# Hymba layer, both feed-forward products: seven block products in both halves, the second one product by product over all channels, weight sums stored

## The chip, the cores and the metric

One core of a Trainium2 chip. The metric is device time in microseconds for one execution of the whole program; lower is better. Before the change three runs gave a median of 2140.09 us.

## What is computed (the reference, cut)

One decoder layer over 2048 tokens (16 meta tokens are put ahead and removed again), model width 1024, all in float32:

```python
s = layer_norm(concat(meta, x), ln_in_g, ln_in_b)
u = s @ w_in                       # columns: conv value, conv gate, q, k, v, output gate, forget gate
conv_out = silu(layer_norm(depthwise_conv31(val * sigmoid(gate)) + conv_b))   # 512 channels
gla_out  = rms_norm(gated_linear_attention(q, k, v, log_g)) * silu(r)         # 4 heads, chunks of 64
s = layer_norm(ALPHA * s + concat(conv_out, gla_out) @ w_out, ln1_g, ln1_b)
f = square(relu(s @ w_ff1)) @ w_ff2          # 1024 -> 4096 -> 1024
out = layer_norm(ALPHA * s + f, ln2_g, ln2_b)
```

## The kernel before, in words

**Precision.** TensorE multiplies in a reduced float32 form. Each operand is therefore split into a high part (a cast on ACT, L189) and the rest (a subtraction on DVE, L190), and each product is three matmuls, high by high, high by low, low by high, that add up in one PSUM bank.

**Tiling.** The tokens are four sub-blocks s = 0..3 of 512; two of them are a *half* (half 0 is s = 0, 1; half 1 is s = 2, 3). The order on the chip is: input projection, attention and convolution of all four; then for each half the output projection (`wout_units`), the first feed-forward product (FF1 below) and the second (FF2). `stats`/`late` are the sums of a layer norm whose application is put off into FF1.

**FF1.** An ordinary product of one half is 2 x 2 blocks by 2 x 2 blocks, eight block products. Half 0 does these (`ff1_units`, `ff1_unit`): 16 groups of 256 channels, 4 units each of 24 matmuls of 128x512, 1536 in all. `put_left` then forms the seven left operands that FF2 wants, already split, and stores them (`hod`). Half 1 uses the scheme with seven block products and more additions (`ff1s_units`): 16 groups x 7 products x 12 matmuls, 1344. There products 1 and 2 of the first ten groups (NFR = 10, "the front") run ahead while a side generator (`back_units`) makes the operands X3 to X7 of the others; product 1 of each front group is kept in SBUF (`a1`, 10 buffers), and the seven left operands of FF2 are stored unsplit (`hor`).

**FF2.** In both halves seven block products (`ff2_units`). The 4096 inner channels are four groups q; a *block* is one product i of one group, with i in the order 1, 7, 5, 6, 2, 3, 4, so that there are 28 blocks, and in each 4 units (tt, 128 tokens each) of 12 matmuls: 48 per block, 1344 per half. Before, the blocks run group by group: each unit starts a new bank, and every bank is at once added into accumulators in SBUF (112 evacuations a half, L1251, L1253, L1256). The residual ALPHA*s is added in at the first group. The right operands are the quadrants of w_ff2 (11, 12, 21, 22), loaded once per group (`raw_load`, L1185) and combined in place by 32 DVE subtractions a half (`sub`, L1202). Left operands come from `hod` (half 0) or are loaded from `hor` (`raw_left`, L1159 for blocks 0 and 1, L1163 for later ones) and split (`load_left`, half 1).

**What sets the order.** `prog.add` makes units with a cost; `prog.load` hands weight tiles out of a ring of 10 slots of 512 KB (pool `wp`, tiles `wr`, `w1r`, `wop`); `prog.side` spreads the steps of a generator between two marks, by cost; `prog.defer` puts a step off. A scheduler then fixes each engine's order when the program is built, and the engines run that order: an instruction that waits holds all behind it on its engine. Loads are issued by SP; some stores by ACT. The convolution of sub-block s, `conv(s)`, is such a side generator: 120 `scalar_tensor_tensor` on DVE (L729) with a layer norm over channels, which needs 32 transposes on TensorE (L736, L750).

Of the kernel before, what the change touches and what calls it, by code (L numbers as in the profile page):

```python
# [10 lines left out]
F32 = mybir.dt.float32  # L11
# [134 lines left out]
def hymba_kernel(ctx: ExitStack, tc: tile.TileContext, x, meta, ln_in_g, ln_in_b, w_in, small, gate_up,  # L146
# [639 lines left out]
    def load_ln2():  # L786
        for nm_, src in (("g2", ln2_g), ("b2", ln2_b)):
# [95 lines left out]

    def put_left(half, g, i, t):
        o = B.f1.tile([P, 2, SUB], F32R, tag="ho", name="ho", bufs=6)
        split(o[:, 0, :], o[:, 1, :], t)
        nc.sync.dma_start(out=hod[half][g // GP][i - 1][:, g % GP, :, :].bitcast(F32), in_=o.bitcast(F32))

    hr = {}

    def ff1_unit(s, g, m, ls):
        half, i = divmod(s, 2)
        ps = mm_tile()
        ch_matmul(ps, ls, m, lambda k, hl: xs(st1[s], k, hl))
        t = hr[i, m] = B.f1.tile([P, SUB], F32, tag="hr", name="hr", bufs=8)
        nc.scalar.activation(t, ps, AF.Relu)  # L898
        nc.scalar.activation(t, t, AF.Square)
        if i == 0:  # L900
            put_left(half, g, 1 + m, t)
        if (i, m) == (1, 1):
            a11, a12, a21, a22 = hr[0, 0], hr[0, 1], hr[1, 0], hr[1, 1]
            put_left(half, g, 4, a22)
            s3 = B.f1.tile([P, SUB], F32, tag="s3", name="s3", bufs=2)
            sub = lambda o, x, y: nc.vector.tensor_tensor(out=o, in0=x, in1=y, op=ALU.subtract)
            sub(s3, a11, a21)
            put_left(half, g, 7, s3)
            nc.vector.tensor_tensor(out=a21, in0=a21, in1=a22, op=ALU.add)
            put_left(half, g, 5, a21)  # L910
            sub(a21, a21, a11)
            put_left(half, g, 6, a21)
            sub(a21, a12, a21)
            put_left(half, g, 3, a21)

    def ff1_units(half, tail):
        for g in range(NG):
            l1 = loads_ch(w1, g * G * P)
            for i in range(2):
                for m in range(G):  # L920
                    prog.add(lambda s=2 * half + i, g=g, m=m, l1=l1: ff1_unit(s, g, m, l1), l1, 5.2)
                if i == 0 and g == NG - 1:
                    tail()

# [64 lines left out]
    def ff1s_units(half, stats, f2):  # L989
# [61 lines left out]
        def put(g, i, t, late=False):  # L1051
            o = hor[g // GP][i - 1][:, g % GP, :]
# [9 lines left out]
        bank = {}  # L1062

        def unit(g, i, l):
# [5 lines left out]
            st = bank  # L1070
            if i == 1:
                a1[g] = B.f1.tile([P, SUB], F32, tag="a1", name="a1", bufs=10)
                nc.scalar.copy(a1[g], ps)
            elif i == 2:
# [43 lines left out]
        prog.add(open_h, cost=0.01)  # L1118
# [13 lines left out]
        prog.add(lambda: open_x(True), cost=0.01)  # L1132
        f2.head2()
# [3 lines left out]
    def op_tile(n, r):  # L1137
        if n % 5 == r:
            return B.x.tile([P, GP, 2, SUB], F32R, tag="ox", name="ox")
        return xtp.tile([P, GP, 2, SUB], F32R, tag="xt", name="op")  # L1140

    def ff2_units(half, f2):
        seq = [(q, i) for q in range(NGR) for i in ORDER]
        lt, rt, accs, sums, raws = {}, {}, {}, {}, {}
        count = [0]

        def nxt():
            count[0] += 1
            return op_tile(count[0] - 1, 4 if half else 2)

        stage = {}

        def raw_left(n):
            if half and n < len(seq):
                q, i = seq[n]
                if n < 2:
                    stage[n] = [B.f1.tile([P, SUB], F32, tag="a1", name="lr", bufs=10) for _ in range(GP)]
                    for p in range(GP):
                        nc.sync.dma_start(out=stage[n][p], in_=hor[q][i - 1][:, p])  # L1159
                else:  # L1160
                    stage[n] = [B.acc.tile([P, 2, SUB], F32, tag="lr", name="lr", bufs=4) for _ in range(GP // 2)]
                    for u in range(GP // 2):
                        nc.sync.dma_start(out=stage[n][u], in_=hor[q][i - 1][:, 2 * u:2 * u + 2])  # L1163

        def load_left(n):
            if half:
                if n < len(seq):
                    lt[n] = nxt()
                    for u, r in enumerate(stage[n]):
                        w = GP // len(stage[n])  # L1170
                        o = lt[n][:, u * w:(u + 1) * w]
                        split(o[:, :, 0, :], o[:, :, 1, :], r.rearrange("p (k t) -> p k t", k=1) if w == 1 else r)
            elif n < len(seq):
                q, i = seq[n]
                lt[n] = nxt()
                for p in range(GP):
                    nc.sync.dma_start(out=lt[n][:, p].bitcast(F32), in_=hod[half][q][i - 1][:, p].bitcast(F32))

        def raw_load(q, j, k, u):
            def fn():  # L1180
                t = wp.tile([P, 2, 512], F32, tag="w", name="wr")
                if j is not None:
                    r0 = (q * GP + 2 * u) * G * P
                    src = w2[r0:r0 + 2 * G * P, k * 512:(k + 1) * 512]
                    nc.sync.dma_start(out=t, in_=src.rearrange("(a j p) c -> j p a c", a=2, j=2)[j])  # L1185
# [3 lines left out]
        def group_loads(q):  # L1189
            r = raws[q] = {}  # L1190
            for nm_, j, k in (("11", 0, 0), ("22", 1, 1), ("12", 0, 1), ("t3", None, None), ("21", 1, 0)):
                r[nm_] = [raw_load(q, j, k, u) for u in range(2)]

        needs = {1: ("11",), 7: ("22", "12", "t3"), 5: ("12", "11"), 6: ("22", "12"), 2: ("21",), 3: ("22",),
                 4: ("21", "12")}

        def right(n):
            q, i = seq[n]
            rt[n] = nxt()
            for u in range(2):  # L1200
                b11, b22, b12, t3, b21 = [prog.slot.get(raws[q][x][u]) for x in ("11", "22", "12", "t3", "21")]
                sub = lambda o, x, y: nc.vector.tensor_tensor(out=o, in0=x, in1=y, op=ALU.subtract)  # L1202
                if i == 7:
                    sub(t3, b22, b12)
                elif i == 5:
                    sub(b12, b12, b11)
                elif i == 6:
                    sub(b12, b22, b12)
                elif i == 4:
                    sub(b12, b21, b12)  # L1210
# [216 lines left out]
```

## Time and profile before

| | |
|---|---|
| three runs | 2137.29, 2140.09, 2142.95 us |
| the profiled execution | 2142.86 us, of which the trace's span is 2140.9 us (1.96 us lie around it) |
| TensorE busy | 2061.7 us, 96% of the span |
| DVE, ACT busy | 1639.6 us (77%), 970.4 us (45%) |
| DMA | 391.05 MB, mean 183 GB/s |

The profile names, for each engine, the share of time in which it had an instruction in flight. Matmuls overlap each other, so that the pace of TensorE is read from the distance of their starts, not from their durations. The first matmuls of the stages lie at: FF1 of half 0 713 us, its FF2 1073 us, output projection 2 and 3 1394 us, FF1 of half 1 1487 us, its FF2 1809 us; the last matmul starts at 2123.9 us.

### The profile page before, as it was taken

How to read it: one execution, taken by the hardware profiler on the slowest of the kernel's cores; microseconds unless marked ns; L12 is line 12 of the kernel's file. 1: busy time of each engine (PE TensorE's matmuls, PEld its weight loads, DVE VectorE, ACT ScalarE, POOL GpSimd, SP SyncE). 2: the span in 40 equal slices, each digit the busy share in tenths (PEclk: the TensorE clock that was granted, in tenths of full speed). 3: DMA queues.
4: the chain of work that ended last, by engine and by line, in shares of the span. 5: the costliest groups of instructions: out<-in, count | busy, mean ns of one | idle time of the engine just before them, and what ended most of it. 6: DMA issues, size and time to landing. Idle time of an engine off the chain costs nothing. (4 is left out here: it accounts for less than half of the span.)

```text
span 2140.9 us, 26599 instructions
## 1 busy us (share of the span) xinstructions
PE 2061.7 (96%) x9336; PEld 1687.1 (79%) x9336; DVE 1639.6 (77%) x2670; ACT 970.4 (45%) x1688; POOL 92.0 (4%) x104
## 2 busy tenths in 40 slices
PE   6999999999899999999999999899999999999995
PEld 5878878878777788888878788788777788888884
DVE  6699989989988644599645656868878776787888
ACT  3554474653543445655441312244635555533332
POOL 3000100000000000000000000011000000000002
PEclk9999999999999999999999999999999999999998
DMA  5533534434346476656796876547455547744422
GB/s 187 170 106 103 151 112 126 146 98 129 119 152 211 153 256 219 221 215 229 272 366 251 276 263 229 182 144 222 156 181 190 187 141 259 284 151 155 135 79 79
DMA packets 211654, 391.05 MB, mean 183 GB/s; under 512 B 19792, under 2 KB 103984, under 8 KB 211520
## 3 DMA queue, kind: packets, MB, share of 16 engines
q1 hardware_dynamic: 204608, 376.77, 52.4%
q10 hardware_dynamic: 6912, 12.59, 1.6%
q8 instruction: 73, 1.20, 0.2%
q14 instruction: 61, 0.50, 0.1%
HBM read 263.21 MB, written 126.07 MB: 182 GB/s over the span
## 5 line engine op out<-in xcount | busy, mean ns | idle before, releaser
L393 PE MATMUL mm<-xt,wsl 128*128 128x512 f32 x896 | 353.0, 394 | 0.7 <-ACT xt L189 0.7
L395 PE MATMUL mm<-xt,wsl 128*128 128x512 f32 x896 | 352.0, 393 | 0.0
L394 PE MATMUL mm<-xt,wsl 128*128 128x512 f32 x896 | 351.9, 393 | 0.0
L729 DVE SCALAR_TENSOR_TENSOR cacc<-hin,sm,cacc 128x512 f32<-128x512 f32 x480 | 343.6, 743 | 1.6
L189 ACT CAST wsl<-raw 128x512 fp32r<-128x512 f32 x288 | 176.9, 621 | 207.6 <-PE mm L395 57.9
L190 DVE TENSOR_TENSOR wsl<-raw,wsl 128x512 fp32r<-128x512 f32 x284 | 193.4, 689 | 62.1 <-ACT wsl L189 61.4
L1246 PE MATMUL mm<-op 128*128 128x512 f32 x544 | 213.1, 392 | 6.3 <-DVE aa L1253 6.3
L1247 PE MATMUL mm<-op 128*128 128x512 f32 x544 | 213.2, 392 | 0.9 <-DVE op L190 0.9
L1248 PE MATMUL mm<-op 128*128 128x512 f32 x544 | 212.9, 391 | 0.0
L189 ACT CAST op<-wr 128x1024 fp32r<-128x1024 f32 x92 | 92.5, 1050 | 263.7 <-PE mm L1248 151.7
L393 PEld LDWEIGHTS mm<-xt,wsl 128*128 128x128 f32 x896 | 169.2, 189 | 35.0 <-ACT xt L189 0.9
L394 PEld LDWEIGHTS mm<-xt,wsl 128*128 128x128 f32 x896 | 169.2, 189 | 34.8 <-issue 0.8
L395 PEld LDWEIGHTS mm<-xt,wsl 128*128 128x128 f32 x896 | 169.0, 189 | 34.9
L190 DVE TENSOR_TENSOR op<-wr,op 128x1024 fp32r<-128x1024 f32 x92 | 109.0, 1220 | 39.3 <-ACT op L189 39.3
L1246 PEld LDWEIGHTS mm<-op 128*128 128x128 f32 x544 | 102.8, 189 | 28.3 <-issue 6.7
L1247 PEld LDWEIGHTS mm<-op 128*128 128x128 f32 x544 | 102.7, 189 | 22.8 <-DVE op L190 1.3
L1248 PEld LDWEIGHTS mm<-op 128*128 128x128 f32 x544 | 102.7, 189 | 21.4
L190 DVE TENSOR_TENSOR ho<-hr,ho 128x512 fp32r<-128x512 f32 x96 | 64.5, 684 | 34.9 <-ACT ho L189 32.1
L242 POOL TENSOR_TENSOR rs<-rs,nhalf 128x1 f32<-128x1 f32 x46 | 41.7, 908 | 1120.3 <-DVE rs L241 1117.1
L1251 DVE TENSOR_TENSOR ac<-ac,mm 128x512 f32<-128x512 f32 x72 | 49.1, 683 | 49.3 <-PE mm L1248 49.3
L898 ACT ACTIVATE hr<-mm 128x512 f32<-128x512 f32 x64 | 38.3, 598 | 103.3 <-PE mm L395 103.3
L1246 PE MATMUL mm<-op,ox 128*128 128x512 f32 x192 | 76.3, 397 | 7.6 <-issue 5.4
(304 smaller groups left out, 4362.6 us busy)
## 6 DMA issues: line engine op xcount, KB each, us to landing
hod<-ho SPq DMA_DIRECT2D x112, 512.0 KB, 3.6
op<-hod SPq DMA_DIRECT2D x88, 512.0 KB, 5.9
raw<-in_w_in_dram SPq DMA_DIRECT2D x160, 256.0 KB, 2.9
wr<-in_w_dram SPq DMA_DIRECT2D x64, 512.0 KB, 5.8
lr<-hor SPq DMA_DIRECT2D x52, 512.0 KB, 4.8
raw<-in_w_dram SPq DMA_DIRECT2D x84, 256.0 KB, 2.9
raw<-in_w_out_dram SPq DMA_DIRECT2D x64, 256.0 KB, 3.6
w1r<-in_w_dram SPq DMA_DIRECT2D x32, 512.0 KB, 5.1
```

Source lines behind the costliest of these rows:

```text
L189: nc.scalar.copy(hi, src)
L190: (eng or nc.vector).tensor_tensor(out=lo, in0=src, in1=hi.bitcast(F32), op=ALU.subtract)
L242: nc.gpsimd.tensor_tensor(out=rs, in0=rs, in1=nhalf[:, :1], op=ALU.pow)
L393: nc.tensor.matmul(ps, wh, mov(k, 0), start=(k == 0), stop=False)
L394: nc.tensor.matmul(ps, wh, mov(k, 1), start=False, stop=False)
L395: nc.tensor.matmul(ps, wl, mov(k, 0), start=False, stop=(k == KD - 1))
L729: nc.vector.scalar_tensor_tensor(out=acc, in0=h[:, j:j + SUB], scalar=wc(j), in1=acc, op0=ALU.mult, op1=ALU.add)
L898: nc.scalar.activation(t, ps, AF.Relu)
L1246: nc.tensor.matmul(ps, lh, rt[n][:, p, 0, :], start=(p == 0), stop=False)
L1247: nc.tensor.matmul(ps, lh, rt[n][:, p, 1, :], start=False, stop=False)
L1248: nc.tensor.matmul(ps, ll, rt[n][:, p, 0, :], start=False, stop=(p == GP - 1))
L1251: add = lambda o, a, b: nc.vector.tensor_tensor(out=o, in0=a, in1=b, op=ALU.add)
```

## The change

- FF1 runs with seven block products in half 0 as well (`ff1s_units` for both halves; `ff1_units`, `put_left` and `hod` go; `hor` exists for both). `wout_units(1)` therefore leaves its layer norm to FF1 (`late[0]`).
- The front's product 1 no longer stays in SBUF: ACT stores it (`a1d`), `a1` has 5 buffers, and `reload(g)` brings it back one group ahead.
- FF2 goes through all four groups of one product before the next product. A bank per tt then collects 4 x 12 matmuls, and is emptied only at the last group: a copy on ACT for products 1, 7, 5; four DVE adds for 6; one DVE add for 2, 3, 4. The residual comes in apart from this (`res_load`, `res_add`).
- The quadrants of w_ff2 no longer stay between products. In half 0 each block loads what it needs (`parts`), one or two pieces, and where there are two, the difference is formed (32 of 128x1024), used, and stored by ACT in DRAM (`td`). Half 1 loads the stored differences.
- Only block 0's left operand is fetched ahead of FF2 (`head`); blocks 1 and 2 follow behind `open_f2`.
- `conv(2)` is spread up to the end of FF1 of half 0, `conv(3)` over FF2 of half 0; before, `conv(2)` ended a little into FF1, and `conv(3)` ran mainly in FF1.
- The gains of the last layer norm are loaded after FF2 of half 0, and the layer norm of sub-block 2 runs between the blocks of the last product.

```diff
-        seq = [(q, i) for q in range(NGR) for i in ORDER]
+        seq = [(i, q) for i in ORDER for q in range(NGR)]
...
+        if half == 0:
+            parts = {1: ("11",), 7: ("22", "12"), 5: ("12", "11"), 6: ("22", "t5"), 2: ("21",), 3: ("22",), 4: ("21", "t6")}
+        else:
+            parts = {1: ("11",), 7: ("t7",), 5: ("t5",), 6: ("t6",), 2: ("21",), 3: ("22",), 4: ("t4",)}
...
+                ops = [prog.slot[l] for l in slots[n][u]]
+                x = ops[0]
+                if len(ops) == 2:
+                    nc.vector.tensor_tensor(out=x, in0=x, in1=ops[1], op=ALU.subtract)
+                split(rt[n][:, 2 * u:2 * u + 2, 0, :], rt[n][:, 2 * u:2 * u + 2, 1, :], x)
+                if len(ops) == 2:
+                    nc.scalar.dma_start(out=td[i][q][u], in_=x)
...
-            ps = mm_tile()
+            if q == 0:
+                bank[tt] = mm_tile()
+            ps = bank[tt]
...
+            if q < NGR - 1:
+                return
             x = accs[tt]
...
+            if i in (1, 7, 5):
+                nc.scalar.copy(x.slot[i], ps)
             elif i == 6:
-                add(o, o, ps)
-                add(o, o, x.slot[1])
...
+                add(x.slot[6], x.slot[1], ps)
+                add(x.slot[7], x.slot[7], x.slot[6])
+                add(x.slot[6], x.slot[6], x.slot[5])
+                add(x.slot[5], x.slot[5], x.slot[7])
...
         def head():
             prog.add(lambda: raw_left(0), cost=0.01)
-            prog.add(lambda: raw_left(1), cost=0.01)
             prog.add(lambda: load_left(0), cost=0.01)
             add_right(0)
...
+                if n == 0:
+                    z(raw_left, 1)
+                    z(raw_left, 2)
...
-        if half:
-            ff1s_units(half, stats, f2)
-        else:
-            ff1_units(half, tail)
+        ff1s_units(half, stats, f2)
...
-    mid = m_ff0 + 30
-    prog.side(later(conv(2), 100), CONV_N, W[3].gv_end, mid)
-    prog.side(later(conv(3), 100), CONV_N, mid, m_f20 + 60)
+    prog.side(later(conv(2), 100), CONV_N, W[3].gv_end, m_f20)
+    prog.side(later(conv(3), 100), CONV_N, m_f20, m_w2 - 4)
```

The order on DVE in the middle of FF2 of half 0. Before (`aa`, `ab`, `ac` are the accumulators, `mm` a bank, `wr` weights as loaded, `op`/`ox` split operands):

```order
L1251 TENSOR_TENSOR aa<-aa,mm 128x512
L1202 TENSOR_TENSOR wr<-wr 128x1024 x2
L1251 TENSOR_TENSOR aa<-aa,mm 128x512
L1202 TENSOR_TENSOR wr<-wr 128x1024 x2
L1251 TENSOR_TENSOR aa<-aa,mm 128x512 x2
L190 TENSOR_TENSOR op<-wr,op 128x2x512 x2
L1251 TENSOR_TENSOR ab<-ab,mm 128x512 x4
```

Now, for one block of product 7 (`lr` is a left operand as loaded, `cacc` the convolution's sum):

```order
L730 SCALAR_TENSOR_TENSOR cacc<-hin,sm,cacc 128x512
L1168 TENSOR_TENSOR wr<-wr 128x1024
L730 SCALAR_TENSOR_TENSOR cacc<-hin,sm,cacc 128x512
L1168 TENSOR_TENSOR wr<-wr 128x1024
L730 SCALAR_TENSOR_TENSOR cacc<-hin,sm,cacc 128x512 x5
L191 TENSOR_TENSOR op<-wr,op 128x2x512 x2
L191 TENSOR_TENSOR op<-lr,op 128x2x512 x2
```

The additions into accumulators are gone from the block; seven convolution steps and two splits of the left operand have come in.

On SP at the passage from FF1 to FF2 in half 1. Before, block 1's left operand (`hor0_6`) follows at once on block 0's (`hor0_0`), far ahead of the stores of FF1's last results:

```order
L1159 DMA lr_15136<-hor0_0_168 128x512
L1159 DMA lr_15137<-hor0_0_168 128x512
L1159 DMA lr_15145<-hor0_6_174 128x512
L1159 DMA lr_15146<-hor0_6_174 128x512
L1159 DMA lr_15147<-hor0_6_174 128x512
L1159 DMA lr_15148<-hor0_6_174 128x512
```

Now block 1's (`hor1_1_0`) stands behind the last of these stores:

```order
L1014 DMA hor1_3_5_194<-h11_15151 128x512
L1014 DMA hor1_3_2_191<-s4_15259 128x512
L1147 DMA wr_15285<-td7_2_0_224 128x1024
L1132 DMA lr_15272<-hor1_1_0_175 128x1024
L1132 DMA lr_15273<-hor1_1_0_175 128x1024
L1132 DMA lr_15276<-hor1_2_0_182 128x1024
L1132 DMA lr_15277<-hor1_2_0_182 128x1024
```

The same stands in half 0 (`hor0_1_0` behind the stores to `hor0_3_...`). The place of block 2's load before is the place of block 1's load now.

On ACT in FF2 of half 0, where the stores to `td` are issued; casts of blocks 5 and 6 (counted from 0), now:

```order
L190 CAST op_9670<-wr_9360 128x2x512
L190 CAST op_9670<-wr_9451 128x2x512
L190 CAST op_9716<-lr_9583 128x2x512
L190 CAST op_9716<-lr_9584 128x2x512
L1171 DMA td7_3_0_226<-wr_9600 128x1024
L1171 DMA td7_3_1_227<-wr_9679 128x1024
L190 CAST op_9753<-wr_9522 128x2x512
L190 CAST op_9753<-wr_9596 128x2x512
L190 CAST ox_9797<-lr_9666 128x2x512
L190 CAST ox_9797<-lr_9667 128x2x512
L1171 DMA td5_0_0_204<-wr_9683 128x1024
L1171 DMA td5_0_1_205<-wr_9762 128x1024
```

Each store stands ahead of the casts of the block before it: `td7_3` (group 3 of product 7) is ahead of the casts from `wr_9522`, which is group 2. Before, ACT issued no stores in FF2, only casts and copies of banks.

## Rows read from the trace of the kernel before

**Rows 1.** The page: TensorE's busy time, and the clock granted in 40 slices.

```profile
PE 2061.7 (96%) x9336; PEld 1687.1 (79%) x9336; DVE 1639.6 (77%) x2670; ACT 970.4 (45%) x1688; POOL 92.0 (4%) x104
PEclk9999999999999999999999999999999999999998
```

**Rows 2.** Busy time by stage: length, PE, PEld, DVE, ACT, POOL, clock, DMA share, GB/s.

```profile
601.00:713.00 112.00, 107.49 (x520) 87.45 (x519) 84.94 (x171) 40.81 (x93) 8.59 (x8) 1.00 0.54 178
713.00:1073.00 360.00, 357.25 (x1604) 294.59 (x1603) 250.80 (x405) 193.32 (x335) 6.37 (x8) 1.00 0.64 231
1073.00:1394.00 321.00, 312.09 (x1375) 256.57 (x1374) 202.76 (x277) 89.23 (x119) 2.20 (x4) 0.99 0.73 258
1487.00:1809.00 322.00, 317.16 (x1376) 253.96 (x1376) 237.35 (x383) 169.62 (x298) 3.49 (x4) 1.00 0.55 185
1809.00:2124.00 315.00, 307.72 (x1344) 253.43 (x1342) 256.31 (x318) 122.33 (x141) 4.62 (x5) 0.99 0.43 149
2124.00:2141.00 17.00, 0.00 (x0) 0.00 (x0) 11.64 (x26) 5.52 (x9) 6.63 (x6) 0.63 0.34 130
```

**Rows 3.** Timeline of TensorE late in FF2 of half 0: start, duration, instruction.

```profile
1361.64 0.39 PE L1247 MATMUL mm<-op 128*128 128x512 f32 x1
...
1365.27 0.39 PE L1248 MATMUL mm<-op 128*128 128x512 f32 x1
1371.11 0.77 PE L1246 MATMUL mm<-op,ox 128*128 128x512 f32 x1 [5.45 <-issue]
1371.67 0.63 PE L1247 MATMUL mm<-op,ox 128*128 128x512 f32 x1
1372.10 0.63 PE L1248 MATMUL mm<-op,ox 128*128 128x512 f32 x1
```

**Rows 4.** TensorE's transposes of a convolution's layer norm, 713 to 1073 us, by line.

```profile
L750 PE MATMUL tp<-ident,cn 128*128 128x128 f32 x16 | 3.4, 280 | 0.5 <-ACT cn L747 0.5
L736 PE MATMUL tp<-ident,cacc 128*128 128x128 f32 x16 | 2.6, 272 | 0.0
```

**Rows 5.** DVE's convolution steps (L729 alone) in FF1 and FF2 of half 0.

```profile
713.00:1073.00 360.00, 84.79 (x120) 1.00 0.64 231
1073.00:1394.00 321.00, 0.00 (x0) 0.99 0.73 258
```

**Rows 6.** Timeline of DVE: two instructions back to back, of 1024 and of 512 columns.

```profile
2099.78 2.35 DVE L190 TENSOR_TENSOR ox<-lr,ox 128x1024 fp32r<-128x1024 f32 x2
...
2108.54 1.41 DVE L258 SCALAR_TENSOR_TENSOR aa<-aa,nm,g 128x512 f32<-128x512 f32 x2
```

**Rows 7.** DMA in the busiest stretch, 1073 to 1150: shares, 2-us slices, landing.

```profile
1073.00:1150.00 77.00, 74.87 (x325) 61.62 (x324) 41.34 (x47) 27.40 (x38) 0.55 (x1) 0.98 0.90 333
...
GB/s 406 306 400 421 383 275 362 266 322 371 389 362 404 415 347 375 402 397 413 403 399 410 409 400 367 148 362 387 403 382 32 172 406 413 98 0 30 294 400 402
...
wr<-in_w_dram SPq DMA_DIRECT2D x10, 512.0 KB, 7.8
```

**Rows 8.** Passage to FF2 of half 1: SP's issues, and the left operand of block 2.

```profile
1816.61 0.32 SPq L1054 DMA_DIRECT2D hor<-s  x1
1817.74 0.38 SPq L1185 DMA_DIRECT2D wr<-in_w_dram  x1
1818.22 0.42 SPq L1163 DMA_DIRECT2D lr<-hor  x1
...
L189 ACT CAST ox<-lr x2: 1049/1050/1052, 1823.1 to 1826.7; 128x1024 fp32r<-128x1024 f32 x2
```

**Rows 9.** FF2 of half 1: TensorE's longest wait, and the stretch behind it.

```profile
PE mm L1246 <- DVE aa L1253: 6.3, 1, 6.3
...
2099.40:2106.20 6.80, 6.80 (x19) 5.39 (x20) 6.80 (x12) 0.00 (x0) 0.00 (x0) 0.61 0.00 0
```

**Rows 10.** Timeline of DVE at the end: last addition from a bank, last two steps.

```profile
2125.99 0.68 DVE L1253 SCALAR_TENSOR_TENSOR ab<-ab,mm 128x512 f32<-128x512 f32 x1
...
2132.23 0.20 DVE L235 TENSOR_SCALAR nm<-sums 128x1 f32<-128x1 f32 x1
...
2136.42 1.40 DVE L260 SCALAR_TENSOR_TENSOR ab<-ab,rs,b 128x512 f32<-128x512 f32 x2
```

**Rows 11.** SP's waits in FF1 of half 1: line, releaser, total, times, longest.

```profile
SPq L1086 <- DMA hor<-h: 34.4, 10, 6.1
```

More of the change, by code (lines that the diff above doesn't have):

```diff
@@ L786, in load_ln2 @@
     def load_ln2():
+        B.pool = ctx.enter_context(tc.tile_pool(name="pb2", bufs=1, side="right", reuse_waits="tile"))
         for nm_, src in (("g2", ln2_g), ("b2", ln2_b)):
@@ L1062, in ff1s_units, with reload, main_start @@
         bank = {}
+        front = [True]
+        def reload(g):
+            a1[g] = B.f1.tile([P, SUB], F32, tag="a1", name="a1", bufs=5)
+            nc.sync.dma_start(out=a1[g], in_=a1d[half][g])
+            h11[g] = B.f1.tile([P, SUB], F32, tag="h11", name="h11", bufs=3)
+            nc.sync.dma_start(out=h11[g], in_=hor[half][g // GP][0][:, g % GP, :])
+        def main_start():
+            front[0] = False
+            open_h()
+            reload(0)
         def unit(g, i, l):
@@ L1070, in unit @@
             st = bank
+            if g + 1 < NFR and not front[0] and i == 6:
+                reload(g + 1)
             if i == 1:
-                a1[g] = B.f1.tile([P, SUB], F32, tag="a1", name="a1", bufs=10)
+                a1[g] = B.f1.tile([P, SUB], F32, tag="a1", name="a1", bufs=5)
                 nc.scalar.copy(a1[g], ps)
+                if g < NFR:
+                    nc.scalar.dma_start(out=a1d[half][g], in_=a1[g])
             elif i == 2:
@@ L1142, in ff2_units @@
     def ff2_units(half, f2):
-        seq = [(q, i) for q in range(NGR) for i in ORDER]
-        lt, rt, accs, sums, raws = {}, {}, {}, {}, {}
+        seq = [(i, q) for i in ORDER for q in range(NGR)]
+        lt, rt, accs, slots, stage, bank, res = {}, {}, {}, {}, {}, {}, {}
         count = [0]
@@ L1148, in nxt @@
             count[0] += 1
-            return op_tile(count[0] - 1, 4 if half else 2)
-        stage = {}
+            return op_tile(count[0] - 1)
         def raw_left(n):
[L1154 to L1159, printed above, removed]
+            if n < len(seq):
+                i, q = seq[n]
+                if n == 0:
+                    stage[n] = [B.f1.tile([P, 1, SUB], F32, tag="a1", name="lr", bufs=5) for _ in range(GP)]
@@ L1179, in raw_load, with raw_right @@
-        def raw_load(q, j, k, u):
+            if n < len(seq):
+                i, q = seq[n]
+                lt[n] = nxt()
+                w = GP // len(stage[n])
+                for u, r in enumerate(stage[n]):
+                    o = lt[n][:, u * w:(u + 1) * w]
+                    split(o[:, :, 0, :], o[:, :, 1, :], r)
+        def raw_right(q, nm_, u):
             def fn():
                 t = wp.tile([P, 2, 512], F32, tag="w", name="wr")
-                if j is not None:
+                if nm_[0] == "t":
+                    nc.sync.dma_start(out=t, in_=td[int(nm_[1])][q][u])
+                else:
@@ L1214, in add_right @@
         def add_right(n):
             if n < len(seq):
-                q, i = seq[n]
-                if q not in raws:
-                    group_loads(q)
-                prog.add(lambda: right(n), [raws[q][x][u] for x in needs[i] for u in range(2)], 0.01)
+                i, q = seq[n]
+                slots[n] = [[raw_right(q, nm_, u) for nm_ in parts[i]] for u in range(2)]
+                prog.add(lambda: right(n), slots[n][0] + slots[n][1], 0.01)
         def start():
@@ L1249, in unit @@
+            if tt == 1 and 0 <= n - n_res < TT:
+                res_add(n - n_res)
+            if tt == 2 and 0 <= n + 1 - n_res < TT:
+                res_load(n + 1 - n_res)
+            if half and i == 4 and tt == 2:
+                for _ in ln2(2, q):
+                    pass
+            if q < NGR - 1:
+                return
             x = accs[tt]
-            o = x.slot[i]
             add = lambda o, a, b: nc.vector.tensor_tensor(out=o, in0=a, in1=b, op=ALU.add)
-            last = q == NGR - 1
@@ L1281, in unit @@
                 acc1(o, o, ps, 1.0, to)
-                if half and i != 2:
-                    for _ in ln2(half * 2 + (i == 4), tt):
+                if half and i == 4:
+                    for _ in ln2(3, tt):
                         pass
@@ L1369, in hymba_kernel @@
     prog.add(cvs.close, cost=0.01)
+    prog.add(load_ln2, cost=0.01)
     prog.add(open_w, cost=0.01)
```

205 lines of the change are left out of this document (60 added, 145 removed).

## The prediction

> **What bounds the kernel now.** I read the page first: TensorE is busy 96% of the span and its clock is granted in full in every slice [rows 1]. So the time is the number of matmuls times their pace, plus the stalls. I then cut the span into stages [rows 2], because the change touches three of them in different ways. DMA and DVE differ much between the stages: DMA is at 0.73 in FF2 of half 0 and at 0.43 in FF2 of half 1, DVE at 203 of 321 us and 256 of 315 us.
>
> The pace: the starts at 1361.64 and 1365.27 are 16 matmuls apart [rows 3], 0.227 us each. A block of 48 costs 10.9 us, and 28 blocks 305 us. FF2 takes 321 us in half 0 and 315 us in half 1 [rows 2], so 10 to 16 us there are waits and the clock behind them. The two large ones are a stall of 5.8 us at 1365.5 in half 0 [rows 3] and one of 6.3 us in half 1 [rows 9]. Behind the first, starts lie 0.43 us apart for a while instead of 0.227 [rows 3]: the lower of the two clock levels, 1.2 GHz. That loses some 1.5 us; behind the second the granted clock is 0.61 over 6.8 us [rows 9], which loses about 0.39 x 6.8 = 2.6 us. A stall of six us thus costs 7.5 to 9 us.
>
> **A. FF1 of half 0.** The eight block products are 1536 matmuls, the seven 1344: 192 fewer, at 0.227 some 44 us. But the seven come with work of their own. The same code already runs in half 1 and takes 322 us, against 360 us [rows 2]: 38 us less. Of work which half 1's stage does not have, conv(2)'s layer norm comes in, 32 transposes, busy 3.4 + 2.6 = 6.0 us [rows 4]; as matmuls of 0.39 us start 0.227 apart [rows 3], I take 4. DVE has 237 us of work in half 1's stage; conv(2)'s steps are over before FF1 as they were before, and conv(3)'s 120 steps of 85 us leave this stage [rows 5], so DVE has room for what comes. The front's detour (ten stores by ACT, twenty loads of 256 KB by SP) lies in a stage whose DMA share is 0.55 [rows 2], and is fetched one group (seven products) ahead: I cost it at nothing; were it not covered, see R4. **A = -38 + 4 = -34 us** (-28 if the transposes and their chain cost 10; -37 if they are hidden).
>
> **B. FF2 of half 0.** It has the same 1344 matmuls, 305 us, and the transposes of conv(3)'s norm, 4 us, as conv(3) ended in this stage before too. Gone is the burst at the last group: the four adds per unit for product 6 now read sums that are complete. So the stall at 1365.5 and the clock behind it go (7.3 us). New are two things.
>
> *Block 1's left operand.* It was prefetched before FF2. Now its load stands on SP behind FF1's last stores. In half 1 the load in that place is block 2's: issued at 1818.22, right behind the store at 1816.61, cast from 1823.1 to 1827.7 [rows 8]. FF2's first matmul is at 1808.8, so block 0 ends at 1808.8 + 10.9 = 1819.7. Block 1's first half would be cast and split at about 1825.5, its second at 1829: a wait of 6 us (3 if the stores come earlier without block 0's traffic, 9 if it needs both halves), with the clock behind it 7.5. Queued behind: all of TensorE. Before, block 2 in this place had a block to spare.
>
> *Blocks with two weight pieces.* Sixteen of 28 blocks (products 7, 5, 6, 4) load 1 MB of left operand, four weight pieces of 512 KB and store two: 8 x 0.524 = 4.19 MB in 10.9 us, 385 GB/s. The busiest stretch before shows 333 GB/s at a share of 0.90 [rows 7], so 370 at full share: 11.3 us a block; at 333 flat, 12.6 us. Single slices reach 421, the best sustained value the row shows is some 400. DVE is at its limit as well: two splits of 1024 columns take 2.35 us where one takes 1.22, so 1.13 each in a row, and 512-column steps 1.41 - 0.74 = 0.66 [rows 6]; a block has four splits, two subtractions and seven convolution steps, 6 x 1.13 + 7 x 0.66 = 11.4 us at worst, 11.1 on a mean over twelve blocks (86 steps, 22 subtractions, 50 splits), against 10.9. Neither limit hides the other fully, as loads, subtraction, split and matmul are a chain through a ring of ten slots, of which a block of this kind takes four. I take 11.8, the middle of 11.1 and 12.6: 16 x 0.9 = 14 us (3 to 27). The Trainium skill says on "DMA: Bandwidth & Descriptors", section Bandwidth, that transfers between HBM and SBUF are bound at about 358 GB/s per core by the memory's side; by it a block would take an estimated 11.7 us, the term 13 us instead of 14. The trace shows slices of 400 and more [rows 7], so it is no hard bound here.
>
> Copies at each product's end and small waits, as before: 2 us. **B = 305 + 4 + 7.5 + 14 + 2 = 333, against 321: +12 us** (-8 to +27).
>
> **C. FF2 of half 1 and the end.** Here each block has one weight piece: 1 + 1 MB in 10.9 us, 192 GB/s, no limit, and DVE loses 32 subtractions and 112 - 28 evacuations. The stall and slow clock (6.3 + 2.6) go; block 1's wait comes, 7.5. So 305 + 7.5 = 312.5 against 315: -2.5. At the end the last addition from a bank lies at 2126.0 and the last step ends at 2137.8 [rows 10]; DVE works there in order through the last layer norms, of which the change has done sub-block 2's earlier, all but its last quarter. The last row's own chain (sum, square, scale, store) stays: I take 3 us of 17 off (0 to 5). **C = -5.5 us.**
>
> **D. The rest.** FF1 of half 1 has the same matmuls and now the front's detour: 0 (+-2). The norms' gains are loaded in another place, beside TensorE's work; wout of sub-block 1 leaves its norm to FF1, where `back_units` does it, as half 1's stage includes: 0 (stage 112 us [rows 2]; -2 to +1).
>
> **Sum.** -34 + 12 - 5.5 = -27.5. The profiled execution took 2142.9 us (span 2140.9 and 2.0 around it): 2115.4. That execution lies 2.8 us above the median of the three runs, which is less than the sum's own doubt; I leave 2115.
>
> **The rivals.**
>
> *R1, FF2 of half 0 at TensorE's pace.* DMA reaches 400 GB/s steadily, as many slices do [rows 7], and the ring smooths the rest; the two-piece blocks cost 10.9, and block 1's wait is 3 instead of 6 in both halves. For it: products 1, 2 and 3 need half as much and the ring runs ahead. Against it: DVE's 11.1 to 11.4. Then B is -5, C -8: 2142.9 - 34 - 5 - 8 = 2096, down to 2091 with A at -37 and the end at -5. Chance 0.25.
>
> *R2, bound by the loads.* The steady rate is 333 GB/s, 12.6 us a block, as in the busiest stretch with its gaps [rows 7]: the term is 27 instead of 14, and 2115 + 13 = 2128; with A at -28 2134. For it: that rate was measured with this kind of transfer. Chance 0.22.
>
> *R3, slower: ACT's order.* In half 0 ACT issues the `td` stores, and each waits for DVE's subtraction, which waits for a load, one or two blocks ahead of the casts that stand behind it. Those casts feed TensorE, and the ring's slots come free only with them; so a load that lands late holds up the casts of blocks whose data have long been there, and the loads behind them. A piece takes 7.8 us to land here [rows 7]. If 4 us of it show in each of the 16 blocks beyond my 0.9, that is 16 x 3.1 = 50 us: 2165. It decides from 0.9 + 27.5/16 = 2.6 us per block, a block of 13.5 us. Against it: DMA was this busy before, with TensorE at 74.9 of 77 us [rows 7]. Chance 0.10.
>
> *R4, FF1 of half 0 doesn't gain what half 1's shows.* The front's reload and its stores hold SP: before, SP waited 34.4 us for such a reload, ten times, up to 6.1 each [rows 11], harmlessly, behind TensorE's work. If half of each shows, that is 17 us, in both halves partly: 2130 to 2135. Chance 0.05.
>
> **How the numbers follow.** Forecast 0.38, R1 0.25, R2 0.22, R3 0.10, R4 0.05. The range reaches from R1's lower end, 2091, to 2137, above R2's and R4's; it leaves out R3 and some of the tails, 2 in 10 at most. About 0.3%, 6.4 us, is what a measurement here can tell from no change. Faster needs below 2134: the forecast, R1 and nearly all of R2, 0.83; within it, 0.08 (the rest of R2, most of R4); slower 0.09, R3.
>
> **What the profile after would show.** A: FF1 of half 0 within 323 to 332 us. B: a gap of 3 to 9 us some 11 us after the first matmul of FF2 in both halves, followed by starts 0.43 apart; blocks of products 7, 5, 6 and 4 longer than 10.9 us, those of 2 and 3 not, DMA share near 0.9 in the first; no stall at product 6. C: no wait of 6 us late in half 1, and fewer DVE steps behind the last matmul. Wrong would make me: blocks of 13.5 us or more with TensorE waiting for ACT's casts (R3), or two-piece blocks at 10.9 (R1).

## The result: 2111.5 us instead of 2141.2

Four runs of the changed kernel gave a median of 2111.47 us (2107.91 to 2116.01), four of the kernel before, 2141.23 (2137.29 to 2142.95): a ratio of 0.9865, 95% interval 0.9841 to 0.9889. The change makes the kernel 1.35% faster, and the forecast was 2115. The profiled execution took 2107.91 us, its span is 2106.2; that of the kernel before took 2142.86.

The changed kernel cut into stages, as [rows 2] before (length, busy PE, PEld, DVE, ACT, POOL, clock, DMA share, GB/s). The fourth row is output projection 2 and 3, which took 92.2 us before (1394.4 to 1486.6):

```profile
594.00:706.00 112.00, 108.18 (x523) 87.91 (x522) 85.58 (x172) 41.18 (x93) 8.61 (x8) 1.00 0.52 169
706.00:1033.00 327.00, 319.61 (x1399) 256.01 (x1398) 242.95 (x397) 176.71 (x310) 4.91 (x6) 1.00 0.60 201
1033.00:1357.80 324.80, 314.03 (x1378) 257.91 (x1377) 288.74 (x364) 136.10 (x170) 2.94 (x5) 0.98 0.82 299
1357.80:1457.40 99.60, 95.11 (x430) 76.65 (x429) 73.64 (x150) 48.21 (x83) 13.23 (x14) 0.98 0.67 220
1457.40:1780.50 323.10, 316.09 (x1377) 254.12 (x1376) 239.72 (x390) 169.98 (x298) 3.56 (x4) 1.00 0.60 201
1780.50:2090.20 309.70, 306.48 (x1345) 253.03 (x1343) 167.85 (x201) 119.90 (x135) 5.66 (x6) 0.99 0.57 193
2090.20:2106.20 16.00, 0.17 (x1) 0.00 (x0) 11.44 (x23) 5.02 (x8) 5.62 (x6) 0.65 0.38 145
```

Read against [rows 2]: FF1 of half 0 fell from 360 to 327 us, which is nearly the whole gain. FF2 of half 0 rose from 321 to 325, and its DMA from 258 to 299 GB/s, its DVE from 203 to 289 us. Output projection 2 and 3 lost 7 us. FF2 of half 1 fell from 315 to 310. The stretch ahead of the first row is 6.6 us shorter than before (594.2 against 600.8); in the twelve kernels below, which run the same instructions there, it lies between 596.1 and 601.5, so that much of it is what two executions differ by.

TensorE's waits of more than 1.6 us in these stages: three in FF2 of half 0, one in FF2 of half 1, one in output projection 2 and 3 (line, releaser, total, times, longest).

```profile
PE mm L1219 <- DVE op L191: 4.8, 1, 4.8
PE mm L1218 <- ACT op L190: 3.1, 1, 3.1
PE mm L1218 <- ACT ac L1233: 1.7, 1, 1.7
...
PE mm L1218 <- ACT op L190: 3.2, 1, 3.2
...
PE gl L867 <- DVE wacc L874: 2.4, 1, 2.4
```

The two of 3.1 and 3.2 us are block 1's, in both halves. In half 0, on SP, ACT and TensorE:

```profile
1039.14 2.55 SPq L1132 DMA_DIRECT2D lr<-hor  x4
...
1047.99 1.04 ACT L190 CAST op<-lr 128x1024 fp32r<-128x1024 f32 x1 [4.41 <-DMA lr<-hor]
...
1049.09 0.50 PE L1218 MATMUL mm<-op 128*128 128x512 f32 x1 [3.13 <-ACT op L190]
```

SP issues the load 6.1 us after FF2's first matmul (1033.0), ACT has waited 4.4 us for it to land, and TensorE for the cast. Blocks 0 and 1 together take 28.7 us in half 0 and 26.8 in half 1 (starts of their matmuls), against 21.8 at full pace. In half 0 the last 12 transposes of conv(2)'s norm lie among them.

The wait of 4.8 us lies at block 11 (blocks are counted from 0), the last of product 5; the one of 1.7 us, for a copy of a bank on ACT, at block 12. DVE, SP and ACT ahead of it:

```profile
1155.17 1.23 DVE L1168 TENSOR_TENSOR wr<-wr 128x1024 f32<-128x1024 f32 x1 [0.54 <-DMA wr<-td]
...
1162.44 1.23 DVE L1168 TENSOR_TENSOR wr<-wr 128x1024 f32<-128x1024 f32 x1 [3.81 <-DMA wr<-td]
1163.58 2.35 DVE L191 TENSOR_TENSOR op<-wr,op 128x1024 fp32r<-128x1024 f32 x2
...
1154.00 2.78 ACTq L1171 DMA_DIRECT2D td<-wr  x2
1156.87 2.00 ACT L190 CAST op<-wr 128x1024 fp32r<-128x1024 f32 x2 [9.52 <-DVE wr L1168]
```

DVE waits for a stored sum to come in (twice), for blocks 13 and 14, and behind its subtraction stand, in order, block 11's split, which TensorE needs, and, on ACT, a store to `td` with two of block 11's casts behind it: ACT was idle for 9.5 us although these casts' own data had been subtracted by 1134.4. The casts still came before block 11 began (1159.7); what TensorE waited for in it is DVE's split. Blocks 11 and 12 take 18.4 and 12.9 us; the other two-piece blocks of products 7, 5 and 6 take 10.9. The DMA engines in the stretch up to this:

```profile
1033.00:1076.00 43.00, 39.55 (x172) 32.04 (x171) 36.08 (x48) 24.81 (x36) 1.42 (x2) 0.96 0.97 344
1076.00:1120.00 44.00, 44.00 (x196) 36.43 (x195) 38.65 (x42) 14.53 (x17) 0.00 (x0) 1.00 0.98 370
1120.00:1165.00 45.00, 40.20 (x178) 32.96 (x176) 38.67 (x43) 17.52 (x20) 0.00 (x0) 0.98 1.00 384
```

Their share is 0.97 to 1.00 for 130 us, at a rising rate. That 384 GB/s isn't yet their limit, e3 and e5 show below.

### The profile page after: what moved, and what is told of

It is laid out like the page before. It is cut to its first block, busy times and chain, and to the rows that moved or that the text cites. A ratio compares the mean times of both kernels' runs of the same rounds, so it can differ in the third digit from the quotient of the medians.

```text
span 2106.2 us, 26291 instructions
## 1 busy us (share of the span) xinstructions
PE 2023.0 (96%) x9144; PEld 1647.4 (78%) x9144; DVE 1631.5 (77%) x2642; ACT 1004.5 (48%) x1720; POOL 94.1 (4%) x104
## 5 line engine op out<-in xcount | busy, mean ns | idle before, releaser
L190 ACT CAST wsl<-raw 128x512 fp32r<-128x512 f32 x224 | 136.6, 620 | 160.9 <-DMA raw<-in_w_in_dram 40.2
L191 DVE TENSOR_TENSOR wsl<-raw,wsl 128x512 fp32r<-128x512 f32 x220 | 149.2, 689 | 23.7 <-ACT wsl L190 23.0
L1007 PE MATMUL gl<-x,wop 128*128 128x512 f32 x384 | 152.0, 397 | 5.2 <-DVE u L1041 2.1
L394 PE MATMUL mm<-xt,wsl 128*128 128x512 f32 x384 | 153.0, 399 | 0.0
L395 PE MATMUL mm<-xt,wsl 128*128 128x512 f32 x384 | 151.9, 396 | 0.0
L396 PE MATMUL mm<-xt,wsl 128*128 128x512 f32 x384 | 151.6, 395 | 0.0
L1008 PE MATMUL gl<-x,wop 128*128 128x512 f32 x384 | 150.7, 392 | 0.0
L1009 PE MATMUL gl<-x,wop 128*128 128x512 f32 x384 | 150.1, 392 | 0.0
L1218 PEld LDWEIGHTS mm<-op 128*128 128x128 f32 x544 | 103.5, 190 | 28.7 <-ACT op L190 7.1
L191 DVE TENSOR_TENSOR op<-lr,op 128x1024 fp32r<-128x1024 f32 (+1 forms) x92 | 104.9, 1172 | 25.6 <-ACT op L190 25.6
L190 ACT CAST wop<-w1r 128x512 fp32r<-128x512 f32 x152 | 91.0, 616 | 68.5 <-DVE w1r L978 40.3
L191 DVE TENSOR_TENSOR wop<-w1r,wop 128x512 fp32r<-128x512 f32 x152 | 103.6, 687 | 17.4 <-ACT wop L190 16.8
L1007 PE MATMUL mm<-xt,wop 128*128 128x512 f32 x256 | 100.7, 396 | 4.3 <-ACT a L1047 4.3
L1008 PE MATMUL mm<-x,wop 128*128 128x512 f32 x256 | 101.1, 395 | 1.6 <-DVE x L191 1.6
```

The lines of the kernel that those rows point to most:

```text
L190: nc.scalar.copy(hi, src)
L191: (eng or nc.vector).tensor_tensor(out=lo, in0=src, in1=hi.bitcast(F32), op=ALU.subtract)
L394: nc.tensor.matmul(ps, wh, mov(k, 0), start=(k == 0), stop=False)
L395: nc.tensor.matmul(ps, wh, mov(k, 1), start=False, stop=False)
L396: nc.tensor.matmul(ps, wl, mov(k, 0), start=False, stop=(k == KD - 1))
L1007: nc.tensor.matmul(ps, wh, X[i][:, k, 0, :], start=start and k == 0, stop=False, skip_group_check=not start)
```

## The experiments

Each edit is made to the changed kernel unless another is named. "Stage" lengths are from the starts of matmuls in the profiled execution; medians are of all runs. The median of the kernel before lay between 2141.0 and 2142.0 beside all of them; the ratios are to that.

**e1: FF1 of half 0 undone.**

```diff
-        ff1s_units(half, stats, f2)
+        if half:
+            ff1s_units(half, stats, f2)
+        else:
+            ff1_units(half, tail)
...
```

> FF1 of half 0 goes back to the eight block products (1536 matmuls), with the seven left operands stored unsplit in one piece each; FF2 stays as changed in both halves. Theory (the gain is FF1's 192 matmuls, term A; FF2's two halves and the passages cancel to within a few us): FF1 of half 0 takes 357 to 362 us instead of 327, FF2 of both halves as in the changed kernel, the whole 2111 + 33 = 2144, within 0.3% of the kernel before. Rival (the new order of FF2 carries a good part of the gain): 2125 to 2132, 0.5% or more below the kernel before.

Measured: 2147.54 us, 1.0031 of the kernel before (1.0019 to 1.0042). FF1 of half 0 takes 358.5 us, FF2 of the halves 327.8 and 311.5, output projection 2 and 3 98.6. So the seven products are worth 2147.5 - 2111.5 = 36 us, of which FF1's stage has 31.6 and the two FF2 stages nearly 5, and all the rest of the change together costs about 6. The theory holds. conv(3)'s 120 steps are out of FF1 here too, so the gain doesn't come from the room they leave on DVE.

**e2: block 1's left operand early.**

```diff
+            early[:] = [early_left(u) for u in range(2)]
...
-                    z(raw_left, 1)
```

> Only block 1's left operand is moved: its two loads go through the ring of ten slots behind block 0's weights, so they are issued before the last stores of FF1 instead of behind them. Theory (block 1 waits for this load, and the clock falls behind the wait): the gaps of 3.6 us in both halves and the slow starts behind them go, 5 us in each half: 2111 - 10 = 2101. Rival 1 (DMA is full at the passage of half 0, share 0.97 over 43 us, so what comes earlier pushes another load back): 5 us in half 1, nothing in half 0: 2106. Rival 2 (the wait moves to block 2): no change, 2111.

Measured: 2101.98 us, 0.9819 (0.9805 to 0.9834): 9.5 us less, as the theory had it. FF2 of half 1 runs without a wait, 28 blocks at 10.9 us:

```profile
1778.20:2083.00 304.80, 304.80 (x1345) 251.99 (x1343) 167.76 (x201) 119.95 (x135) 5.74 (x6) 1.00 0.57 196
```

In half 0 blocks 0 and 1 take 23.5 us instead of 28.7; the 1.7 us above the pace that are left are those of conv(2)'s 12 transposes. The stretch with two weight pieces keeps its loss there, in other blocks: 9 to 12 together 9.7 us over the pace. At block 12 it is ACT's order, in this row of the timeline with the bank copies behind a convolution step that waits for its input:

```profile
1178.81 0.81 ACT L727 ACTIVATE cacc<-hin,sm 128x512 f32<-128x512 f32 x1 [3.44 <-DMA hin<-hd]
1179.21 0.39 ACTq L1185 DMA_DIRECT2D td<-wr  x1
1179.53 1.54 ACT L1247 COPY ac<-mm 128x512 f32<-128x512 f32 x3
...
1180.15 0.50 PE L1232 MATMUL mm<-op,ox 128*128 128x512 f32 x1 [2.67 <-ACT ac L1247]
```

**e3: the sums of product 7 not stored.**

```diff
-                if len(ops) == 2:
+                if len(ops) == 2 and half == 0 and i != 7:
                     nc.scalar.dma_start(out=td[i][q][u], in_=x)
...
-            parts = {1: ("11",), 7: ("t7",), ...
+            parts = {1: ("11",), 7: ("22", "12"), ...
```

> The eight sums of product 7 (4.2 MB) are not stored in half 0; half 1 loads their two pieces and subtracts, as half 0 does. Theory (the stall at blocks 11 and 12 of half 0, 5.2 us with slow starts and 2.1 behind it, some 9 us in all, is the DMA engines' lack: twelve blocks of 4.19 MB want 385 GB/s, and 370 to 384 flow): the twelve blocks move 4.2 MB less of 50, at 380 GB/s 11 us of transfer, and the stall goes: FF2 of half 0 about 316 instead of 325, half 1 unchanged within 1 us (289 GB/s in four blocks): 2111 - 8 = 2103. Rival (DVE at 11.1 to 11.4 us a block is what runs late): the stall stays, 2111, or grows in half 1 by its eight new subtractions.

Measured: 2109.41 us, 0.9848 (0.983 to 0.9865). In its profile FF2 of half 0 takes 313.1 us, 11.7 less, and block 11 is back at 10.9. Of the 11.7 us, 7.7 are gained at blocks 11 and 12; the rest lies at blocks 0 and 1, which the edit doesn't touch. And the whole moved by 2 us, within what these runs can tell. In the same profile FF1 of half 0 was 3.6 us longer, and block 1's wait in half 1 2.3 us longer (5.9 instead of 3.6). The first is within the spread of that stage, 326 to 331 us over all kernels here that have it; the second may come from the two weight pieces that are loaded beside block 1's operand, which no run separates. Blocks 8 to 11, which still store their sums, show what the DMA engines can move at TensorE's full pace, 409 GB/s:

```profile
1129.00:1173.00 44.00, 44.00 (x196) 36.44 (x195) 39.60 (x43) 14.97 (x17) 0.00 (x0) 1.00 1.03 409
```

**e4: conv(3) ends four blocks earlier.**

```diff
-    prog.side(later(conv(3), 100), CONV_N, m_f20, m_w2 - 4)
+    prog.side(later(conv(3), 100), CONV_N, m_f20, m_w2 - 32)
```

> Only the end of conv(3)'s side is moved four blocks ahead, from just before the output projection to 28 units earlier, so that its four stores leave SP before the loads of that projection. Theory (output projection 2 and 3 takes 99.6 us instead of 92.2 because SP holds its loads behind conv(3)'s last stores, 1349.9 to 1369.3): that stage goes back to 92 to 93 us, 2111 - 7 = 2104. Rival (the same 120 steps of DVE in 24 blocks instead of 28 make DVE late in the blocks with two weight pieces): FF2 of half 0 grows by 5 us or more, no gain or a loss.

Measured: 2123.52 us, 0.9927 (0.9905 to 0.995): 12 us worse. The projection took 96.2 us instead of 99.6, but FF2 of half 0 335.2. The rival won by its number. Its blocks were others, though: the longest wait lies at block 23, which loads one weight piece, where TensorE's transposes waited for a sum of the convolution that DVE had not finished:

```profile
PE tp L737 <- DVE cacc L730: 7.9, 1, 7.9
```

**e5: each sum stored twice** (the second copy is read by nobody).

```diff
                     nc.scalar.dma_start(out=td[i][q][u], in_=x)
+                    nc.scalar.dma_start(out=td2[i][q][u], in_=x)
```

> Each weight sum of half 0 is stored a second time, to a place nobody reads: a block with two weight pieces moves 5.24 MB instead of 4.19, and DVE, TensorE and the casts have what they had. Theory (the DMA engines' rate is the limit of these blocks, at 370 to 384 GB/s, and the ring's 5 MB are all that lies between): products 7, 5 and 6 take twelve times 13.6 to 14.2 us instead of 10.9, 33 to 40 us more less some 5 for the ring, product 4 about 10 more: FF2 of half 0 takes 360 to 370 us instead of 325. Rival (DVE's steps limit these blocks, DMA has room to spare): less than 10 us more.

Measured: one run of 2139.44 us. FF2 of half 0 takes 347.5 us, 22.7 more: far more than the rival's 10, less than the theory's 35 to 45. The rate says why; the DMA engines had more to give than 384 GB/s:

```profile
1085.00:1139.00 54.00, 49.67 (x210) 40.37 (x209) 44.79 (x48) 18.23 (x22) 0.00 (x0) 0.94 1.04 410
1139.00:1188.00 49.00, 40.77 (x170) 32.64 (x169) 38.58 (x41) 14.84 (x17) 0.00 (x0) 0.94 1.03 413
```

At 410 GB/s a block of 5.24 MB needs 12.8 us, one of 4.19 MB 10.2, less than TensorE's 10.9. The second store also stands in ACT's order and holds its ring slot longer; what that costs, this run doesn't separate.

**e6: conv(3) with 3 of its 30 steps per channel tile.** This kernel leaves out taps 4 to 30 of the taps 0 to 30.

```diff
             for j in range(1, CW):
+                if s == 3 and j > 3:
+                    yield
+                    continue
```

> conv(3) leaves out 27 of its 30 steps per channel tile (108 of 120 on DVE, some 72 us of FF2 of half 0); the rest of it, norm and stores, stays where it is. Theory (DMA limits the blocks with two weight pieces): the stall at blocks 11 and 12 stays as it is, 7 to 10 us, and FF2 of half 0 is no shorter than 319. Rival (DVE limits them): the stall goes, FF2 of half 0 at 314 or less.

Measured: one run of 2109.57 us. DVE's work in FF2 of half 0 falls from 289 to 218 us; the stage takes 319.1 us. Block 11 still takes 15.5 us, block 12 is down to 11.0: 4.7 us lost in place of 9.5.

```profile
PE mm L1222 <- DVE op L191: 2.9, 1, 2.9
```

So the stall needs no full DVE; about half of its length went with the steps, in this one execution.

**e7: e2 and e3 together** (both diffs above).

> Both edits: block 1's left operand early through the ring, and the sums of product 7 not stored. Theory (two separate causes, block 1's wait and the DMA engines' lack at blocks 9 to 12): they add: FF2 of half 0 at 308 to 312 us, of half 1 at 305, the whole 2102 - 8 = 2094. Rival (what e3 saved in half 0 comes back in other stages, as its median showed only 2 of the 11 us): 2100 to 2102.

Measured: 2106.66 us, 0.9835 (0.9819 to 0.9851): nearest the rival. It lies above e2 alone (2101.98), but the two intervals overlap. Block 11 takes 12.1, but block 12 15.4, and 23 and 24 lose 4.6. The waits now are for ACT's bank copies (line, releaser, total, times, longest):

```profile
PE mm L1232 <- ACT ac L1247: 3.7, 2, 2.6
```

The two gains don't add. In e2, with all bytes, the same waits were 4.0 us in two, so once block 1's load is early, fewer bytes no longer take the stall away.

**e8: e7 with conv(3) begun in FF1.**

```diff
-    prog.side(later(conv(2), 100), CONV_N, W[3].gv_end, m_f20)
-    prog.side(later(conv(3), 100), CONV_N, m_f20, m_w2 - 4)
+    prog.side(later(conv(2), 100), CONV_N, W[3].gv_end, m_f20 - 60)
+    prog.side(later(conv(3), 100), CONV_N, m_f20 - 60, m_w2 - 32)
```

> As e7, and conv(3) begins 60 units before the end of FF1 of half 0, where DVE is busy 74% of the time, and ends 28 units earlier than before; conv(2) ends where it begins. Theory (e4 lost because the steps were pressed into fewer blocks while DVE had no time; spread over a longer stretch, both ends are free): no wait of TensorE for the convolution's sums, and output projection 2 and 3 loses the 3 to 7 us that SP's order costs there: 2094 - 5 = 2089. Rival (FF1 has no room on DVE after all, as its own chains wait for it): FF1 of half 0 grows by 5 us or more, 2094 or above.

Measured: 2105.21 us, 0.9834 (0.9819 to 0.9848), no different from e7. FF1 of half 0 took 326.3 us, so it has the room, and the projection took 96.2. But FF2 of half 0 took 329.8: the earlier end again puts the norm's transposes where TensorE waits for them, this time for ACT.

```profile
PE tp L751 <- ACT cn L748: 8.3, 3, 7.4
```

**e9: e2 with conv(3)'s results stored by POOL.**

```diff
-            nc.sync.dma_start(out=mixd[s][0]...
+            (nc.gpsimd if s == 3 else nc.sync).dma_start(out=mixd[s][0]...
```

> e2 with one edit: conv(3)'s four result stores are issued by POOL instead of SP, so that SP's loads for output projection 2 and 3 no longer stand behind them. Theory (that stage's 7 us come from SP's order): the stage goes from 99.4 to 92 to 94 us, the whole 2102 - 6 = 2096. Rival (its inputs arrive late in any case, because the last of conv(3)'s results are themselves among them): 98 us or more, 2102.

Measured: 2105.54 us, 0.9834 (0.982 to 0.9848); the projection takes 100.7 us. The theory, as put, falls: SP has the stores no longer, and waits all the same, for conv(3)'s transposes on TensorE and its last product on DVE (the second group of rows shows SP's waits: line, releaser, total, times, longest).

```profile
1361.07 0.33 SPq L791 DMA_DIRECT2D g<-in_ln_g_dram  x1
1370.32 0.33 SPq L791 DMA_DIRECT2D b<-in_ln_b_dram  x1
1376.29 1.75 SPq L832 DMA_DIRECT2D mraw<-mixd  x4
1378.09 0.43 SPq L840 DMA_DIRECT2D wacc<-s0d  x1
```

```profile
SPq L791 <- PE tp L737: 18.0, 1, 18.0
SPq L791 <- DVE cy L759: 8.9, 1, 8.9
```

In the program next in SP's order come the last norm's gains (`g`, `b`), whose tiles lie in a pool opened where conv(3)'s was closed; `b` goes out 9 us after `g`. Then come the loads of mix 3, which are conv(3)'s results. The residuals (`wacc`) and the rest of the projection's weights stand behind both.

**e10, e11: e2 with the sums stored by POOL, and with both kinds of store by POOL.**

```diff
-                    nc.scalar.dma_start(out=td[i][q][u], in_=x)
+                    nc.gpsimd.dma_start(out=td[i][q][u], in_=x)
```

> e2 with one edit: the stores of the weight sums are issued by POOL instead of ACT, so that no cast or bank copy stands behind a store that waits for DVE's subtraction. Theory (the waits left at blocks 9 to 12 of half 0 are the DMA engines' lack, passed on to TensorE through whatever stands in order): the bytes are the same, so the stalls stay at 7 to 10 us, 2100 to 2103. Rival (ACT's order makes them): they fall to 3 us or less, 2095.

> e2 with both kinds of store issued by POOL. Theory (SP's order costs 6 us at the output projection, the other waits are DMA's): as e9, 2096. Rival (both orders cost): 2088 to 2091. A third way: POOL is late with the small steps of the norms that DVE and ACT wait for, and it is slower than e9.

Measured: 2103.03 us, 0.9816 (0.9802 to 0.9829), for e10, no different from e2; 2107.66, 0.9841 (0.9827 to 0.9854), for e11. In e10 blocks 9 to 12 lose 1.8 us where e2 lost 9.7, as the rival had it, and no wait for ACT's casts or copies is left there. But blocks 13 to 16 lose 5.4, and the stage is only 2 us shorter than e2's. What is left are waits for DVE, for its splits and for the additions of product 6:

```profile
PE mm L1233 <- DVE op L191: 2.0, 2, 1.3
PE mm L1232 <- DVE ac L1245: 1.9, 1, 1.9
```

In e11, with the same stores off ACT, block 9 takes 17.3, with a wait of 3.4 for DVE's split. Its median is no different from e9's, so its three expectations stay undecided.

**e12: e9 with the gains and mix 3 loaded in the middle of output projection 2.**

```diff
-    prog.add(load_ln2, cost=0.01)
+    prog.add(open_ln2, cost=0.01)
...
-    prog.add(lambda: mix_load(3), cost=0.01)
-    wout_units(2)
+    wout_units(2, mid={1: load_ln2, 4: lambda: mix_load(3)})
```

> e9 with one more edit: the loads of the last norm's gains (which go into memory that conv(3) leaves free) and the load of mix 3 (which needs conv(3)'s results) are written not ahead of output projection 2 but after its second and fifth unit, so that five further weight pieces and the four residual tiles go ahead of them on SP, and weight casts ahead of the mix casts on ACT. Theory (what stands in order behind conv(3)'s end is what costs the 7 us there): the stage goes from 100.5 to 92 to 95 us, 2105 - 6 = 2099 or, against e2, 2096. Rival (the weight pieces and residuals aren't what TensorE waits for there; conv(3)'s own steps on DVE and ACT beside the projection's are): 98 us or more.

Measured: 2099.85 us, 0.9804 (0.9788 to 0.982). The projection takes 93.4 us, TensorE busy for 92.7 of them:

```profile
1364.30:1457.70 93.40, 92.67 (x429) 76.11 (x428) 70.22 (x143) 45.17 (x78) 12.53 (x16) 1.00 0.67 220
```

That is 7.3 us off the stage of e9, and 5.7 off its median. So what stood in order behind conv(3)'s end was the cost of that stage; which of the two loads, the run doesn't separate. It is the fastest of the twelve, but against e2 it gains only 2 us, within the intervals, where 6 were expected.

## Why the prediction was right, point by point

**A, FF1 of half 0: -34, measured -33 in the profile, -32 by e1's stage.** The stage was forecast at 326 us, from half 1's 322 and 4 for the convolution's transposes, and took 326.9; 20 of conv(2)'s 32 transposes lay in it, the others in FF2's first two blocks. The front's detour cost nothing that can be seen: FF1 of half 1, which has it too, went from 322.2 to 323.1.

**B, FF2 of half 0: +12, measured +3.** Both new costs came, and both smaller; the first at the place and by the chain that were named, the second by another chain than the forecast's. The stage is 305 us of matmuls, 6.9 at blocks 0 and 1, 9.5 at blocks 11 and 12, and 3.6 of conv(3)'s transposes at the end.
- Block 1's wait: forecast 6 us and 7.5 with the clock behind it. The waits were 3.6 us between matmuls in each half, some 5 with the slow starts. SP issued the load 6.1 us after FF2's first matmul in half 0 and 7.9 in half 1, where [rows 8] had 9.4, because the stores of FF1's last results came earlier too. e2 shows that the load's place is the cause: moved, it gives 9.5 us in two halves.
- Blocks with two weight pieces: forecast 14 us as 0.9 on each of sixteen. Measured 9.5, all at blocks 11 and 12; twelve of the sixteen blocks took 10.9 us, which the prediction itself had named as a sign of being wrong (R1). The step that was mis-sized is the rate: I divided the mean of [rows 7] by its share, 333/0.90 = 370 GB/s, so that every block had to be late. The engines give 409 (e3) and 410 (e5), at which a block's bytes take 10.2 us and fit. The other limit, DVE at 11.1 to 11.4 us a block, rested on seven convolution steps in each; there were 36 from 1083 to 1160 us, in seven blocks, and from 1076 to 1120 DVE was busy for 38.7 of 44 us. What is left is a chain: a piece lands late, and the subtraction, the store and the casts behind it pass the delay on. That is like R3's mechanism, but at block 11 the order that TensorE waited for was DVE's, a split behind a subtraction, and not ACT's; and it showed once, not sixteen times, far from R3's 50 us. That this term came near is luck.

The Trainium skill's sentence on the 358 GB/s of the memory's side ("DMA: Bandwidth & Descriptors", section Bandwidth) would have given 13 us for this term. The trace of this kernel, which runs on one core, disagrees with the sentence: 410 and 413 GB/s over 54 and 49 us (e5).

e3, e7, e10 and e11 each ease one link of the chain, and FF2 of half 0 stays at 313 to 321 us with the loss at changing blocks. One profile of each tells little here: e2, e9 and e12, which have the same code up to the last blocks of that stage, took 319.8, 318.7 and 323.1 us. With ACT's order eased, blocks 9 to 12 lost 1.8 us (e10) or 6.4 (e11), so a stall doesn't need it. Which link is the last one these runs don't settle; nor is it settled why e7 gained nothing on e2.

**C, FF2 of half 1 and the end: -5.5, measured -6.** The old stall at product 6 is gone, block 1's wait came, 309.7 us against 312.5 forecast. At the end 16.0 us remain of 17; I had taken 3 off. The last row's own chain, which I named, is what the end consists of: from the end of the last addition from a bank (2092.9) to that of the last step (2103.0) 10.1 us pass, against 11.2 before (2126.7 to 2137.8 [rows 10]).

```profile
2092.19 0.68 DVE L1189 SCALAR_TENSOR_TENSOR ac<-ac,mm 128x512 f32<-128x512 f32 x1
...
2101.59 1.40 DVE L261 SCALAR_TENSOR_TENSOR ac<-ac,rs,b 128x512 f32<-128x512 f32 x2
```

**D, the rest: 0, measured -6.6 and +7.4.** The first is, for the most part, the stretch ahead of the output projections that differs from execution to execution. The second I missed. I saw that the gains' load was moved and that conv(3) ended just before the projection, and costed both at nothing without asking what stands behind them on SP. That is the term that the prediction had wrong. SP in the changed kernel:

```profile
1349.91 19.35 SPq L760 DMA_DIRECT2D mixd<-cy  x4
1369.36 0.57 SPq L791 DMA_DIRECT2D g<-in_ln_g_dram  x1
1370.05 0.37 SPq L791 DMA_DIRECT2D b<-in_ln_b_dram  x1
1371.54 3.60 SPq L832 DMA_DIRECT2D mraw<-mixd  x4
1375.19 0.43 SPq L840 DMA_DIRECT2D wacc<-s0d  x1
```

For 19 us SP does nothing but wait for conv(3)'s four results; mix 3, the residuals (`wacc`) and all but the first six of the projection's weight pieces are loaded later. Before, conv(3)'s last transposes started at 1208.7 us, long ahead of this place. e4 took away a part, 3 us of the stage, and lost more in FF2; e9 took away another and gained nothing. e12 moved all of it, and the stage's 7 us came back, though only 2 of them show against e2.

**The sum.** The parts were -34, +12, -5.5 and 0; in the profile they are -33, +3, -6 and +1, which makes -35, of which 6.6 are the first stretch's. The medians moved by 29.8, the profiles without that stretch by 28. R1 (2096) lay as far off on the one side as R2 (2128) on the other; R4 did not happen. Part of the nearness is luck: B was 9 us too dear, and the projection's 7 us were not in the sum; the two nearly cancel.

## What to carry to other kernels

Fewer matmuls are worth less than their count: 192 at 0.227 us are 44 us, and FF1 gained 33. A stage of the same kernel that already runs the scheme, with its own work hidden, was the best price list here. When work is moved to the end of a stage, list what stands behind its last store on the issuing queue, into whose memory the next loads go, and who reads its result: here the three together delayed the next stage, and taking away one alone gained little or nothing. For a DMA limit, take the rate from slices at full share, not the mean divided by the share, and look for the shortage at single blocks, where a store, a subtraction or a cast stands in order behind a late load.

## What the runs showed of the hardware

The sixteen DMA engines of this one core kept 410 GB/s for 54 us and 413 for 49 (e5), and 409 for 44 us with TensorE at full pace (e3), with loads by SP and stores by ACT mixed; the busiest 77 us before had a mean of 333 [rows 7]. The same instructions ahead of the first output projection took between 594.2 and 601.5 us in fourteen profiled executions, not all on one chip, and FF1 of half 0 with seven products 326 to 331: there, single profiles compare stages to some 5 us, not to 1. FF2 of half 1 without block 1's wait, where TensorE never waits, took 304.7 us in each of seven kernels (e2, e7 to e12).
